# Feed-forward's first projection by seven block products in a float32 four-layer block

## The chip, the cores and the metric

One core of a Trainium2 chip runs one program. The time is device microseconds of that core for one execution, from a fixed set of inputs in device memory. An engine here is one of TensorE (PE, with its weight loads PEld), VectorE (DVE), ScalarE (ACT), GpSimd (POOL) and SyncE (SP), each with its own queue that is worked off in order; transfers are issued from such a queue too. TensorE's granted clock is 1.00 at 2.4 GHz and 0.50 at 1.2 GHz.

## The reference

The input is 512 tokens of 1024 channels. Four layers follow each other, each a mixer and a gated feed-forward with residuals and root-mean-square norms: a short convolution with forgetting attention, a conformer convolution, a gated recurrence in chunks, and windowed attention with sinks. The feed-forwards have the inner width 2816; layers 0 and 1 are plain, layers 2 and 3 put a causal convolution of three taps over the gate ahead of its silu.

```
def swiglu_ffn(h, w_ffn_in, w_ffn_out):
    g, u = jnp.split(h @ w_ffn_in, 2, axis=-1)
    return (jax.nn.silu(g) * u) @ w_ffn_out
```

All matrices are float32.

## The kernel before, in words

Every product of float32 matrices is made of three passes over float32r halves: each operand x is split into a high half (a ScalarE copy with rounding) and a low half (VectorE: x less the high half), and `mm3` (L539 to 541) adds high by high, high by low and low by high into one PSUM bank. The normed input lies transposed in `xh` and `xl` (8 blocks of 128 channels by 512 tokens).

Weights come as 379 units of 128 by 1024 numbers (512 KB) in the order of use: `w_dma` (issued at L484) loads a unit from SP's queue up to eight ahead, `w_hi` (L498, ScalarE) and `w_lo` (L507, VectorE) split it, and `get_w` hands the halves out. A unit of the up-projection holds all 1024 input channels of 128 output channels: `fm_unit` runs eight blocks of `mm3` with 512 token columns for it. Per feed-forward there are 22 pairs of such units (gate and value). The first two pairs go through `fm_quads(4)`: first the left 256 tokens of all four units, then the right 256, so that TensorE has work while the norm of the last token blocks is still under way. After each pair `epi` takes silu of the gate (L792, or L797 to L804 with the convolution), multiplies it with the value (L805) and splits the product (L530, L531) for the second projection, `out_proj`, which keeps TensorE busy for 22 more units.

At a stage's end `boundary` spawns for each of four token blocks the residual, the norm and `pre_norm`: ScalarE squares, VectorE scales, TensorE transposes (`xt`, L689), then the split into `xh` (L698) and `xl` (L699).

Nothing of the order is written by hand: each piece of work is a generator with a priority. A planner keeps a clock for each engine and takes at each step the operation that can start first, ties going to the smaller priority; its costs are in the code (`dve`, `act`, `pe`, `dma`, with `LAT` between engines). The order that it gives each engine is the order of that engine's queue on the chip. Buffers come from pools that the planner also counts: 34 slots of 4 KB a partition, 8 small tiles of 512 columns, 8 PSUM banks. Where the planner finds a hole of TensorE of over 0.6 us it puts in `warm` matmuls.

## Time and profile before

| | us |
|---|---|
| median of 3 runs (2326.45 to 2327.47) | 2326.93 |
| the profiled execution | 2326.68 |
| its span, first to last instruction | 2324.9 |
| TensorE busy | 2306.1 (99%) |
| VectorE busy | 1197.4 (52%) |
| ScalarE busy | 912.1 (39%) |
| POOL busy | 134.8 (6%) |

Stretches in the span: layer 0's feed-forward has its two plain pairs from 236 to 261 us, 20 pairs to 478.5, the second projection to 601; layers 1, 2 and 3 have the same stretches from 784, 1432 and 1955 us. Durations of single instructions overlap with their neighbours' on the same engine; the step from start to start is what one costs in a full queue. "[0.26 <-ACT wh L498]" behind a row says that the engine had been idle for 0.26 us and what released it.

### The profile page before, as it was taken

What the parts mean: (1) busy time and instruction counts of PE and PEld (TensorE: products, weight loads), DVE (VectorE), ACT (ScalarE), POOL (GpSimd) and SP (SyncE); (2) the same over time, 40 slices, a digit from 0 to 9 for tenths busy, and PEclk for the clock granted to TensorE, in tenths of its full rate; (3) what the DMA queues carried; (4) which work ended last, traced back from release to release, by engine and by line L of the source; (5) the groups of instructions that cost most, each with busy time, mean ns of one, the idle gap of its engine ahead of it and who ended that gap; (6) DMA issues with size and microseconds to landing.
All of it is one profiled execution on the core that took longest, in us unless ns stands there. A gap on an engine that the chain in (4) does not pass through costs nothing.

```text
span 2324.9 us, 29594 instructions
## 1 busy us (share of the span) xinstructions
PE 2306.1 (99%) x11888; PEld 1969.2 (85%) x11888; DVE 1197.4 (52%) x2038; ACT 912.1 (39%) x1614; POOL 134.8 (6%) x162
## 2 busy tenths in 40 slices
PE   9999999999999999999999999999999999999998
PEld 9888988888978988888888888888888998888887
DVE  5786433333687633333564875444434655444432
ACT  6454323222466322323443444333322664333321
POOL 0000000000284000000000000000000000000000
PEclk9999999999999999999999999999999999999999
DMA  4223322233333222234121214222243022222340
GB/s 179 101 82 118 119 73 91 81 128 107 120 138 126 91 91 76 90 106 154 73 73 64 73 47 135 91 73 77 96 163 109 19 90 93 91 73 76 105 137 36
DMA packets 62936, 224.68 MB, mean 97 GB/s; under 512 B 6984, under 2 KB 7240, under 8 KB 62800
## 3 DMA queue, kind: packets, MB, share of 16 engines
q1 hardware_dynamic: 62368, 222.41, 27.9%
q8 instruction: 93, 1.52, 0.3%
q10 hardware_dynamic: 432, 0.40, 0.1%
q14 instruction: 43, 0.35, 0.0%
HBM read 220.67 MB, written 2.11 MB: 96 GB/s over the span
## 4 chain that ended last, share of the span: by engine, by line
PE 95%; POOL 1%; DVE 1%; ACT 1%; issue 1%; DMA 0%; SPq 0%; POOLq 0%; ACTq 0%
PE fm L539 18%; PE fm L540 18%; PE fm L541 18%; PE op L539 9%; PE op L541 9%; PE op L540 9%; PE tm L539 2%; PE tm L541 2%; PE tm L540 2%; POOL cy L1190 1%; PE xt L689 1%; PE O L1745 1%; PE S L1508 1%; PE o L1571 1%; PE PT L1734 1%
## 5 line engine op out<-in xcount | busy, mean ns | idle before, releaser
L539 PE MATMUL fm<-xh,wh 128*128 128x512 f32 (+1 forms) x2160 | 794.8, 368 | 0.0
L540 PE MATMUL fm<-xl,wh 128*128 128x512 f32 (+1 forms) x2160 | 787.3, 364 | 0.2 <-DVE xl L699 0.2
L541 PE MATMUL fm<-xh,wl 128*128 128x512 f32 (+1 forms) x2160 | 787.3, 364 | 0.0
L507 DVE TENSOR_TENSOR wl<-wr,wh 128x1024 fp32r<-128x1024 f32 x379 | 457.4, 1232 | 287.2 <-ACT wh L498 182.3
L498 ACT ACTIVATE wh<-wr 128x1024 fp32r<-128x1024 f32 x379 | 387.6, 1052 | 264.0 <-DMA wr<-wall 138.5
L541 PEld LDWEIGHTS fm<-xh,wl 128*128 128x128 f32 x2160 | 407.9, 189 | 65.3
L539 PEld LDWEIGHTS fm<-xh,wh 128*128 128x128 f32 x2160 | 408.3, 189 | 61.7
L540 PEld LDWEIGHTS fm<-xl,wh 128*128 128x128 f32 x2160 | 408.3, 189 | 61.4 <-DVE xl L699 0.4
L539 PE MATMUL op<-wh,p 128*128 128x512 f32 x704 | 274.9, 390 | 0.4 <-DVE sg L805 0.4
L541 PE MATMUL op<-wh,p 128*128 128x512 f32 x704 | 274.0, 389 | 0.0
L540 PE MATMUL op<-wl,p 128*128 128x512 f32 x704 | 273.9, 389 | 0.0
L805 DVE TENSOR_TENSOR sg<-fm,sg 128x512 f32<-128x512 f32 x88 | 60.9, 692 | 383.2 <-PE fm L541 376.1
L530 ACT ACTIVATE p<-sg 128x512 fp32r<-128x512 f32 x88 | 55.6, 632 | 357.4 <-DVE sg L805 357.4
L539 PEld LDWEIGHTS op<-wh,p 128*128 128x128 f32 x704 | 132.1, 188 | 28.1 <-DVE sg L805 0.9
L541 PEld LDWEIGHTS op<-wh,p 128*128 128x128 f32 x704 | 132.1, 188 | 27.7
L540 PEld LDWEIGHTS op<-wl,p 128*128 128x128 f32 x704 | 132.2, 188 | 27.0
L660 POOL TENSOR_TENSOR ss<-ss,mhalf 128x1 f32<-128x1 f32 x48 | 26.0, 541 | 1417.1 <-DVE ss L655 1417.0
L539 PE MATMUL op<-wh,y 128*128 128x512 f32 x256 | 102.7, 401 | 0.2 <-DVE y L1004 0.2
L541 PE MATMUL op<-wh,y 128*128 128x512 f32 x256 | 100.0, 391 | 0.0
L540 PE MATMUL op<-wl,y 128*128 128x512 f32 x256 | 99.8, 390 | 0.0
L531 DVE TENSOR_TENSOR p<-sg,p 128x512 fp32r<-128x512 f32 x88 | 60.9, 692 | 61.4 <-ACT p L530 61.4
L1190 POOL TENSOR_TENSOR cy<-cp,cy 128x512 f32<-128x512 f32 x60 | 86.1, 1434 | 30.2 <-ACT cp L1189 26.3
(247 smaller groups left out, 2269.9 us busy)
## 6 DMA issues: line engine op xcount, KB each, us to landing
wr<-wall SPq DMA_DIRECT2D x379, 512.0 KB, 3.6
row<-rows SPq DMA_DIRECT2D x14, 512.0 KB, 3.9
cm<-cmat SPq DMA_DIRECT2D x14, 512.0 KB, 4.0
h<-x SPq DMA_DIRECT2D x8, 256.0 KB, 6.6
nck<-negc SPq DMA_DIRECT2D x4, 512.0 KB, 5.1
alibi<-alibi SPq DMA_DIRECT2D x4, 512.0 KB, 4.4
out<-out SPq DMA_DIRECT2D x8, 256.0 KB, 2.1
mk<-masks SPq DMA_DIRECT2D x2, 288.0 KB, 5.3
```

The lines of the kernel that those rows point to most:

```text
L498: yield act(1024, lambda: A.activation(out=b.t, in_=r.t, func=AF.Copy), (r,), (b,))
L507: yield dve(1024, lambda: V.tensor_tensor(out=b.t, in0=r.t, in1=hh.t.bitcast(F32), op=ALU.subtract), (r, hh), (b,))
L530: yield act(n, lambda: A.activation(out=y0, in_=raw, func=AF.Copy), (rb,), (yb,), psum=psum)
L531: yield dve(n, lambda: V.tensor_tensor(out=y1, in0=raw, in1=y0.bitcast(F32), op=ALU.subtract), (rb,), (yb,))
L539: T.matmul(out, lhsT=a[0], rhs=b[0], start=s, stop=False)
L540: T.matmul(out, lhsT=a[0], rhs=b[1], start=False, stop=False)
L541: T.matmul(out, lhsT=a[1], rhs=b[0], start=False, stop=e)
L660: yield Op("POOL", 0.29 + 0.167 * cols, lambda: G.tensor_tensor(out=ss[:, 8:8 + cols], in0=ss[:, 4:4 + cols], in1=mhalf[:, :cols], op=ALU. ...
L689: T.transpose(b[:, 128 * i:128 * i + 128], n[:, c:c + 128], ident)
L805: yield dve(512, lambda: V.tensor_tensor(out=c.t, in0=u.t, in1=c.t, op=ALU.mult), (u, c), (c,))
L1190: yield pool(512, lambda: G.tensor_tensor(out=y.t, in0=p.t, in1=y.t, op=ALU.add), (p,), (y,))
L1508: T.matmul(b[:, 128 * i:128 * i + 128].rearrange("p (j l) -> p j l", l=ln), lhsT=mix[:, 128 * i:128 * i + 128], rhs=dims(QP, 256 * i + ln, ...
```

## The change

In 20 of 22 pairs the product of a pair (gate and value, both 1024 channels by 128 outputs) with the input is treated as a product of two-by-two blocks: tokens in halves, channels in halves. Seven products of 512 channels by 256 tokens replace eight. Three of the seven need single weight blocks (11, 21, 22), four need sums of weight blocks (t1 to t4), and four need sums of input blocks, which `x_sums` makes at the start of each feed-forward from float32 copies that `keep` saves. `seven_sums` makes the weight sums in float32 and splits each of the seven: the first two sums come by one transfer from POOL's queue that adds 512 KB from DRAM (`wadd`) onto the unit in SBUF; the third sum is a VectorE addition, the fourth too in layers 0 and 1, and in layers 2 and 3 a second adding transfer of 256 KB. `pair` runs the products, `epi7` puts the outputs together from four PSUM banks, then comes `epi`. The product is now kept in float32 and split during the second projection (`halves`). Units of these pairs are loaded six ahead. The planner's price of `mm3` changes from 3 x 0.000422 a column to 3 x (0.0135 + columns / 2400) everywhere.

```diff
     def ffn(wi, wo):
         for m in range(NF):
-            us.append(_fm(wi, 128 * m))
-            us.append(_fm(wi, FF + 128 * m))
+            g, v = _fm(wi, 128 * m), _fm(wi, FF + 128 * m)
+            if m < N_PLAIN:
+                us.extend((g, v))
+            else:
+                us.append(np.concatenate([g[:, :512], v[:, :512]], 1))
+                us.append(np.concatenate([g[:, 512:], v[:, 512:]], 1))
...
+def weight_sums(a):
+    return np.stack([_fm(w, FF + 128 * m) for w in (a["w_ffn_in"][0], a["w_ffn_in"][1], a["ffn_w_up_2"][0], a["ffn_w_up_2"][1])
+                     for m in range(N_PLAIN, NF)])
...
+N_PLAIN = 2
+FFN_AT = (33, 33 + 3 * NF + 24, 33 + 6 * NF + 64, 33 + 9 * NF + 82)
+SEVEN = {u for f in FFN_AT for u in range(f + 2 * N_PLAIN, f + 2 * NF)}
+AHEAD_SEVEN = 6
...
     def w_dma():
         for u in range(N_UNITS):
             state["dma"] = u
-            yield Wait(lambda: u < W.cur + W.ahead_dma)
-            b = yield Alloc(spool, [128, 1024], F32, "wr", low=lambda: 4 if len(W.raw) > len(W.lo) + W.gone else 2)
-            yield dma(524288, lambda: nc.sync.dma_start(out=b.t, in_=ap["wall"][u]), (), (b,))
+            yield Wait(lambda: u < W.cur + (AHEAD_SEVEN if u in SEVEN else W.ahead_dma))
+            b = yield Alloc(spool, [128, 1024], F32, "wr", low=lambda: 1 if u in SEVEN else 4 if len(W.raw) > len(W.lo) + W.gone else 2)
+            yield dma(524288, lambda: nc.sync.dma_start(out=b.t, in_=ap["wall"][u]), (), (b,), lat=2.6 if u in SEVEN else 2.0)
             W.raw[u] = b
-
+            if u in SEVEN and u % 2 != SEVEN_ODD:
+                seven_sums(u - 1)
...
+    def seven_sums(u):
+        s1, s2 = W.raw[u], W.raw[u + 1]
+        f = max(i for i in range(4) if FFN_AT[i] <= u)
+        n = f * (NF - N_PLAIN) + (u - FFN_AT[f]) // 2 - N_PLAIN
+        subs = []
+        def part(s):
+            x = Buf(name="wsum", need=0)
+            x.w, x.weng = s.w, "DMA"
+            subs.append((s, x))
+            return x
+        l1, r1, l2, r2 = part(s1), part(s1), part(s2), part(s2)
+        left = [3]
+        lo_, hi_ = slice(0, 512), slice(512, 1024)
+        def piece(name, src, x):
+            b = yield Alloc(spool, [128, 2, 512], F32R, "w" + name, need=2, low=lambda: 0 if u < W.cur + 2 else 1)
+            yield act(512, lambda: A.activation(out=b[:, 0, :], in_=src, func=AF.Copy), (x,), (b,))
+            yield dve(512, lambda: V.tensor_tensor(out=b[:, 1, :], in0=src, in1=b[:, 0, :].bitcast(F32), op=ALU.subtract), (x,), (b,))
+            W.piece[u, name] = b
+        def end():
+            left[0] -= 1
+            if left[0] == 0:
+                for s, x in subs:
+                    s.r = max(s.r, x.r)
+                    s.w = max(s.w, x.w)
+                free(s1, s2)
+                W.gone += 2
+        def third():
+            yield from piece("t3", s1[:, hi_], r1)
+            end()
+        def first():
+            yield from piece("11", s1[:, lo_], l1)
+            yield Op("POOL", 1.0, lambda: G.dma_start(out=s1.t, in_=ap["wadd"][n], accum_op=ALU.add), (), (l1, r1), lat=6.5)
+            S.spawn(third(), prio, "sum3")
+            yield from piece("t1", s1[:, lo_], l1)
+            yield dve(512, lambda: V.tensor_tensor(out=s1[:, lo_], in0=s1[:, lo_], in1=s2[:, hi_], op=ALU.add), (r2,), (l1,))
+            yield from piece("t2", s1[:, lo_], l1)
+            if f > 1:
+                yield Op("POOL", 1.0, lambda: G.dma_start(out=s1[:, lo_], in_=ap["wall"][u + 1][:, lo_], accum_op=ALU.add), (), (l1,), lat=5.0)
+            else:
+                yield dve(512, lambda: V.tensor_tensor(out=s1[:, lo_], in0=s1[:, lo_], in1=s2[:, lo_], op=ALU.add), (l2,), (l1,))
+            yield from piece("t4", s1[:, lo_], l1)
+            end()
+        def second():
+            yield Wait(lambda: u < W.cur)
+            yield from piece("22", s2[:, hi_], r2)
+            yield from piece("21", s2[:, lo_], l2)
+            end()
+        def prio():
+            return -8 if u < W.cur + 2 else 1 + 0.001 * u
+        S.spawn(first(), prio, "sum1")
+        S.spawn(second(), prio, "sum2")
...
+    def pass3(n):
+        return 3 * (0.0135 + n / 2400.0)
...
+            if len(blocks) > 4:
+                S.spawn(keep(b, tb, kh, blocks[4]), -9.5 + tb, "keep")
+            else:
+                free(b)
...
+    def keep(b, tb, kh, raws):
+        if tb not in raws:
+            raws[tb] = yield slot((128, 2, 512), F32, "xr", need=2)
+        r = raws[tb]
+        yield act(512, lambda: A.activation(out=r[:, kh, :], in_=b.t, func=AF.Copy), (b,), (r,), psum=True)
+        free(b)
+    def x_sums(raws):
+        yield Wait(lambda: 2 in raws)
+        for i in range(4):
+            X.sums[i] = ((yield slot((128, 4, 256), F32R, "xs", need=2)), (yield slot((128, 4, 256), F32R, "xs", need=2)))
+        def one(t):
+            yield Wait(lambda: t in raws and t + 2 in raws)
+            a, b = raws[t], raws[t + 2]
+            x = yield t2("xd")
+            a11, a12, a21, a22 = a[:, 0, :], a[:, 1, :], b[:, 0, :], b[:, 1, :]
+            ba, bb, ts_ = Buf(name="xa", need=0), Buf(name="xb", need=0), slice(128 * t, 128 * t + 128)
+            def parts(i, src, rd):
+                h_, l_ = X.sums[i]
+                src = src.rearrange("p (k t) -> p k t", t=128)
+                oh, ol = h_[:, :, ts_], l_[:, :, ts_]
+                yield act(512, lambda: A.activation(out=oh, in_=src, func=AF.Copy), (rd,), (h_,))
+                yield dve(512, lambda: V.tensor_tensor(out=ol, in0=src, in1=oh.bitcast(F32), op=ALU.subtract), (rd, ), (l_,))
+            yield dve(512, lambda: V.tensor_tensor(out=x.t, in0=a11, in1=a21, op=ALU.subtract), (a, b), (x,))
+            yield dve(512, lambda: V.tensor_tensor(out=a21, in0=a21, in1=a22, op=ALU.subtract), (b,), (bb,))
+            yield dve(512, lambda: V.tensor_tensor(out=a22, in0=a21, in1=a11, op=ALU.subtract), (a, bb), (bb,))
+            yield dve(512, lambda: V.tensor_tensor(out=a12, in0=a12, in1=a22, op=ALU.add), (a, bb), (ba,))
+            yield from parts(0, a21, bb)
+            yield from parts(2, x.t, x)
+            free(x)
+            yield from parts(1, a22, bb)
+            yield from parts(3, a12, ba)
+            a.r = max(a.r, ba.r)
+            b.r = max(b.r, bb.r)
+            free(a, b)
+        for t in range(2):
+            S.spawn(one(t), -7, "xsum")
...
     def ffn(conv, R, chain_of):
-        ps = {}
-        spool.reserve += NF
+        at = W.cur
+        assert at in FFN_AT
+        pr, pp = {}, {}
+        left = [NF // 2]
+        spool.reserve += 1
+        def prod(b, cs, u, name, mov, rd):
+            yield Wait(lambda: (u, name) in W.piece)
+            w = W.piece.pop((u, name))
+            for k in range(4):
+                sl = slice(128 * k, 128 * k + 128)
+                yield pe(pass3(256), lambda: mm3(b[:, cs], (w[:, 0, sl], w[:, 1, sl]), mov(k), k == 0, k == 3), [w] + rd, [b])
+            free(w)
+        def block(half, kh):
+            ts_ = slice(256 * half, 256 * half + 256)
+            return (lambda k: (xh[:, 4 * kh + k, ts_], xl[:, 4 * kh + k, ts_])), [X.blocks[2 * half + i][kh] for i in range(2)]
+        def total(i):
+            a, b = X.sums[i]
+            return (lambda k: (a[:, k, :], b[:, k, :])), [a, b]
+        L_, R_ = slice(0, 256), slice(256, 512)
+        def pair(m):
+            u = at + 2 * m
+            yield Wait(lambda: (u, "11") in W.piece)
+            W.cur += 2
+            a = yield bank("fa", need=8)
+            yield from prod(a, L_, u, "11", *block(0, 0))
+            yield from prod(a, R_, u, "t1", *total(0))
+            b = yield bank("fb", need=8)
+            yield from prod(b, L_, u, "t3", *total(2))
+            yield from prod(b, R_, u, "22", *total(3))
+            d = yield bank("fd", need=4)
+            S.spawn(epi7(m, a, b, d, cs := []), -6, "epi7")
+            yield from prod(d, L_, u, "t2", *total(1))
+            c = yield bank("fc", need=8)
+            cs.append(c)
+            yield from prod(c, L_, u, "21", *block(0, 1))
+            yield from prod(c, R_, u, "t4", *block(1, 1))
+        def epi7(m, a, b, d, cs):
+            x = yield t2("x7", need=0)
+            v = yield t2("v7", need=0)
+            yield act(256, lambda: A.activation(out=x[:, L_], in_=a[:, L_], func=AF.Copy), (a,), (x,), psum=True)
+            yield dve(256, lambda: V.tensor_tensor(out=x[:, R_], in0=d[:, L_], in1=x[:, L_], op=ALU.add), (d, x), (x,))
+            free(d)
+            yield dve(256, lambda: V.tensor_tensor(out=v[:, L_], in0=a[:, R_], in1=x[:, R_], op=ALU.subtract), (a, x), (v,))
+            free(a)
+            yield dve(256, lambda: V.tensor_tensor(out=x[:, R_], in0=b[:, L_], in1=x[:, R_], op=ALU.add), (b, x), (x,))
+            yield dve(256, lambda: V.tensor_tensor(out=v[:, R_], in0=v[:, L_], in1=b[:, L_], op=ALU.subtract), (b, v), (v,))
+            yield dve(256, lambda: V.tensor_tensor(out=v[:, L_], in0=b[:, R_], in1=v[:, L_], op=ALU.add), (b, v), (v,))
+            free(b)
+            yield Wait(lambda: cs)
+            c = cs[0]
+            yield dve(512, lambda: V.tensor_tensor(out=x.t, in0=c.t, in1=x.t, op=ALU.add), (c, x), (x,))
+            free(c)
+            yield from epi(m, x, v)
...
-            yield dve(512, lambda: V.tensor_tensor(out=c.t, in0=u.t, in1=c.t, op=ALU.mult), (u, c), (c,))
-            free(u)
-            p = yield slot((128, 2, 512), F32R, "p", need=2)
-            spool.reserve -= 1
-            yield from split(c.t, c, (p[:, 0, :], p[:, 1, :]), p)
-            free(c)
-            ps[m] = p
-
-        bs = yield from fm_quads(4)
-        S.spawn(epi(0, bs[0], bs[1]), -5, "epi")
-        S.spawn(epi(1, bs[2], bs[3]), -5, "epi")
-        for m in range(2, NF):
-            g = yield from fm_unit()
-            u = yield from fm_unit()
-            S.spawn(epi(m, g, u), -5, "epi")
+            j = m // 2
+            if j not in pr:
+                pr[j] = None
+                pr[j] = yield slot((128, 2, 512), F32, "p", need=2)
+                left[0] -= 1
+                if left[0] < 1:
+                    spool.reserve -= 1
+            yield Wait(lambda: pr[j] is not None)
+            p = pr[j]
+            yield dve(512, lambda: V.tensor_tensor(out=p[:, m % 2, :], in0=u.t, in1=c.t, op=ALU.mult), (u, c), (p,))
+            free(u, c)
+        def halves():
+            for m in range(NF):
+                yield Wait(lambda: at + 2 * NF + m < W.cur + 3 and pr.get(m // 2) is not None)
+                p = pr[m // 2]
+                y = yield slot((128, 2, 512), F32R, "ph", need=2)
+                yield from split(p[:, m % 2, :], p, (y[:, 0, :], y[:, 1, :]), y)
+                pp[m] = y
+                if m % 2:
+                    free(p)
+        if len(X.blocks) > 4:
+            S.spawn(x_sums(X.blocks[4]), -7, "xsums")
+        bs = yield from fm_quads(2 * N_PLAIN)
+        for i in range(N_PLAIN):
+            S.spawn(epi(i, bs[2 * i], bs[2 * i + 1]), -5, "epi")
+        S.spawn(halves(), -5, "halves")
+        yield Wait(lambda: len(X.sums) == 4)
+        for m in range(N_PLAIN, NF):
+            yield from pair(m)
+        for i in range(4):
+            free(*X.sums[i])
+        X.sums.clear()
         chain, blocks = chain_of()
-        yield from out_proj([lambda m=m: ps.get(m) for m in range(NF)], chain, R)
+        yield from out_proj([lambda m=m: pp.get(m) for m in range(NF)], chain, R)
         X.blocks = blocks
```

## Rows read from the trace of the kernel before

**Rows 1.** The page, parts 1 and 4: busy time of TensorE, ending chain by engine.
```profile
PE 2306.1 (99%) x11888; PEld 1969.2 (85%) x11888; DVE 1197.4 (52%) x2038; ACT 912.1 (39%) x1614; POOL 134.8 (6%) x162
...
PE 95%; POOL 1%; DVE 1%; ACT 1%; issue 1%; DMA 0%; SPq 0%; POOLq 0%; ACTq 0%
```

**Rows 2.** Busy time by windows: us, each engine's us (instructions), granted clock, DMA share, GB/s.
```profile
236.00:261.00 25.00, 25.00 (x211) 24.96 (x210) 13.29 (x20) 10.60 (x19) 1.62 (x3) 1.00 0.44 148
261.00:478.50 217.50, 217.50 (x962) 180.09 (x961) 74.62 (x81) 62.71 (x80) 0.00 (x0) 1.00 0.26 87
478.50:601.00 122.50, 122.50 (x555) 101.65 (x554) 47.22 (x56) 36.69 (x56) 3.24 (x6) 1.00 0.33 110
...
1457.00:1674.50 217.50, 217.50 (x961) 180.10 (x961) 102.45 (x117) 79.04 (x100) 0.00 (x0) 1.00 0.24 83
...
1980.00:2197.50 217.50, 217.50 (x962) 180.09 (x962) 102.44 (x117) 77.46 (x98) 0.00 (x0) 1.00 0.25 84
```

**Rows 3.** Order of time, TensorE, 300.4 to 301.4 us: start, us; four more lie between.
```profile
300.21 0.39 PE L541 MATMUL fm<-xh,wl 128*128 128x512 f32 x1
...
301.35 0.39 PE L540 MATMUL fm<-xl,wh 128*128 128x512 f32 x1
```

**Rows 4.** Waits of 261 to 478.5 us: who, for whom, total us, times, longest.
```profile
DVE sg L805 <- PE fm L541: 119.4, 20, 6.2
...
DVE p L531 <- ACT p L530: 14.0, 20, 0.8
```

**Rows 5.** Order of time, TensorE: a half-width matmul, and the first full-width one after.
```profile
250.18 0.28 PE L539 MATMUL fm<-xh,wh 128*128 128x256 f32 x1
...
260.98 0.40 PE L539 MATMUL fm<-xh,wh 128*128 128x512 f32 x1
```

**Rows 6.** VectorE and ScalarE one by one: the input's split by tile, then order of time.
```profile
L699 DVE TENSOR_TENSOR xl<-xt,xh x64: 675/684/692, 11.4 to 1963.4; 128x512 fp32r<-128x512 f32 x64
...
225.53 1.28 DVE L699 TENSOR_TENSOR xl<-xt,xh 128x512 fp32r<-128x512 f32 x2
...
1190.05 0.41 DVE L1552 TENSOR_TENSOR QK<-QK,T 128x256 f32<-128x256 f32 x1
...
1191.05 0.76 DVE L1553 TENSOR_TENSOR QK<-QK,T 128x256 f32<-128x256 f32 x2
...
621.63 3.38 DVE L1164 SCALAR_TENSOR_TENSOR cy<-u,pf,cy 128x512 f32<-128x512 f32 x5
625.16 0.75 DVE L1134 SCALAR_TENSOR_TENSOR u<-fm,pf,sg 128x512 f32<-128x512 f32 x1
...
248.76 2.96 ACT L498 ACTIVATE wh<-wr 128x1024 fp32r<-128x1024 f32 x3
...
263.58 2.36 DVE L507 TENSOR_TENSOR wl<-wr,wh 128x1024 fp32r<-128x1024 f32 x2 [0.26 <-ACT wh L498]
```

**Rows 7.** Busy time by windows, columns as in rows 2: a stretch of the convolution module.
```profile
616.00:660.00 44.00, 44.00 (x233) 37.91 (x231) 39.96 (x56) 26.49 (x40) 31.04 (x23) 1.00 0.24 80
```

**Rows 8.** VectorE in order of time, and TensorE's waits over the span.
```profile
248.42 1.29 DVE L699 TENSOR_TENSOR xl<-xt,xh 128x512 fp32r<-128x512 f32 x2 [2.43 <-ACT xh L698]
...
PE fm L540 <- DVE xl L699: 0.2, 1, 0.2
```

**Rows 9.** The page, part 6: DMA issues, count, size, median us from issue to landing.
```profile
wr<-wall SPq DMA_DIRECT2D x379, 512.0 KB, 3.6
...
nck<-negc SPq DMA_DIRECT2D x4, 512.0 KB, 5.1
```

**Rows 10.** Windows around TensorE's longest wait, columns as in rows 2, and matmuls after it.
```profile
669.70:674.90 5.20, 0.02 (x1) 0.00 (x0) 2.70 (x4) 0.00 (x0) 4.96 (x5) 0.78 0.02 9
674.90:679.00 4.10, 4.08 (x12) 3.41 (x13) 2.50 (x7) 2.92 (x6) 0.90 (x2) 0.50 0.22 66
...
676.70 0.63 PE L541 MATMUL fm<-xh,wl 128*128 128x512 f32 x1
677.12 0.63 PE L539 MATMUL fm<-xh,wh 128*128 128x512 f32 x1
```

41 lines of the change are left out of this document (23 added, 18 removed).

## The prediction

> **What bounds the kernel now.** I read the page first: TensorE is busy for 99% of the span and the chain that ended last is 95% TensorE [rows 1]; VectorE has 52% and ScalarE 39%. Busy time of pipelined matmuls says little, so I looked at starts. In the first feed-forward's up-projection (261 to 478.5 us) the 512-column matmuls follow each other without a hole, 962 of them in the 217.50 us of that row [rows 2], 0.227 us from start to start [rows 3]. Nobody waits for VectorE there to the cost of TensorE: in the list of waits of this stretch VectorE and ScalarE wait for TensorE and for each other, and TensorE is on no line as a waiter [rows 4]. The third and fourth up-projections show the same row, 217.50 us filled, with VectorE busy 102.4 us there and 74.62 us in the first [rows 2]. So this stage is worth exactly its matmuls' spacing, and a change is worth what it takes off that spacing until another engine takes over. The profiled execution took 2326.68 us (span 2324.9 us), 0.25 below the median of the three runs; I sum against 2326.7.
>
> **TensorE's part.** The change leaves two of 22 channel pairs as they are and turns the other 20, in four layers, from 48 matmuls of 512 columns into 7 products x 4 blocks x 3 = 84 matmuls of 256 columns. The old pair costs 48 x 0.2266 = 10.88 us (217.5 us over 20 pairs [rows 2]). The price of a 256-column matmul stands in the trace, because the first two pairs already run in such halves: from 250.18 to 260.98 us there are 90 of them, 0.120 us each, with a weight load in front of every one [rows 5]. The new pair then costs 84 x 0.120 = 10.08 us. The gain is 0.80 us a pair, 7.3% instead of the 12.5% that seven for eight promises, since 84 matmuls pay the part that doesn't shrink with the columns (0.120 - 0.227/2 = 0.0065 us over half a long one) more often than 48. Over 80 pairs: 64 us. The bounds are narrow: 0.119 to 0.121 gives 57 to 71 us.
>
> The Trainium skill, VectorE: DVE Perf Modes, section "The TRN2 errata", prices a matmul at max(60, 6 + columns) cycles, which at the 2.4 GHz that the granted clock of 1.00 stands for is 0.216 and 0.109 us, and would make the gain 48 x 0.216 - 84 x 0.109 = 1.2 us a pair, an estimate of 97 us. The trace differs at both widths (0.227 and 0.120), and the measurement decides.
>
> **VectorE's part.** What a pair asks of it: seven differences of 512 columns (the low halves of the seven blocks), additions of weight blocks (two of 512 in layers 0 and 1, one in layers 2 and 3 where a second transfer replaces it), in the new epilogue five of 256 and one of 512, the product of 512, and in layers 2 and 3 the two convolution steps. It loses two differences of 1024 columns and the split of the product, which moves to the second projection (22 x 0.60 = 13 us a layer, under 122.5 us of matmuls in which VectorE is busy 47 us [rows 2]: nothing). Prices are steps between starts, not durations, since neighbours overlap: two of 512 columns from PSUM take 1.28 us with 0.684 for one, so 0.60 [rows 6]; 256 columns 0.34 (two in 0.76 with 0.41 for one [rows 6]); a step of the convolution's kind 0.66 (five in 3.38 with 0.75 for one [rows 6]). Layers 0 and 1: 7 x 0.60 + 2 x 0.60 + 5 x 0.34 + 0.60 + 0.60 = 8.3 us a pair, 82% of 10.08. Layers 2 and 3: 4.2 + 0.6 + 1.7 + 0.6 + 0.6 + 1.3 = 9.0 us, 89%. ScalarE has seven copies of 512 (about 0.5, half of a large one, three of which take 2.96 [rows 6]), a small one and one or two for the gate: 4.5 to 5.5 us, half the pair. So TensorE stays the bound, but by 1 to 2 us a pair instead of 5 to 7. Is 89% workable for an engine that takes its queue in order? One stretch shows it: from 616 to 660 us VectorE is busy 39.96 of 44 us and TensorE has no hole [rows 7]. There its work is long convolution sums from one buffer, here it is chains across ScalarE, so I don't take the waits as nothing. Bounds for layers 2 and 3: from 0 to 0.7 us a pair (below), I take 0.15, nearer the dense stretch: 40 x 0.15 = 6 us.
>
> The Trainium skill, VectorE: DVE Perf Modes, section "The TRN2 errata", also gives 120 + columns cycles at 0.96 GHz for a VectorE operation that reads PSUM, an estimate of 0.39 us for each of the five epilogue steps and 0.66 for the last, together 0.3 us a pair more, which would bring layers 2 and 3 to 9.3 us, 92%. The trace speaks for less: the pair of 512 columns from PSUM steps at 0.60, not 0.66.
>
> **The entry of each feed-forward.** New there, per layer: eight ScalarE copies that keep the transposed input in float32, four additions and four splits for each of two block rows, thus 16 x 0.60 = 9.6 us of VectorE and 16 x 0.5 = 8 us of ScalarE. They need the last block of the input, whose split ends at 249.7 us in layer 0, and the second product needs them 1.4 us after the plain pairs end at 260.98 [rows 5, 8]. In 236 to 261 us VectorE is busy 13.29 us and ScalarE 10.60 [rows 2]; with 9.6 for the sums and 5.4 for the first pair's blocks, less 4.9 us (three old weight differences and two splits) it comes to 23.4 of 25 us. It fits on paper, with nothing over. The copies and sums stand in the queues beside the norm of the last block; the second half of the plain pairs wants that block about when it is ready now (0.2 us of wait in the whole trace [rows 8]), so what delays it is paid at once. Behind a late sum on VectorE stand the epilogue of the plain pairs and the first pairs' blocks. Bounds per layer: 0 (all in the gaps) to 6 us (half of the sums, 4.8, and one copy pair, 1.0, in front of the norm). I take 2.5: 10 us.
>
> **The transfers.** Each pair adds a 512 KB accumulating transfer on POOL's queue (80 in all), and in layers 2 and 3 one of 256 KB (40). The trace has no accumulating transfer and none from POOL. Nearest rows: a plain 512 KB load lands after 3.6 us, the slowest kind of that size in the table after 5.1 [rows 9]; reading both operands doubles the shortest to 7.2. I take 5 to 7. A pair's blocks are loaded up to three pairs (30 us) ahead, and its chain (first block's split 1.2, transfer 7, split 1.2, addition 0.6, split 1.2, second transfer 6, split 1.2) is 18 us, so it hides; POOL is idle in the stage (0.00 us [rows 2]). Traffic goes from 1 MB in 10.9 us (83 to 87 GB/s, a quarter of the engines' time [rows 2]) to at most 1.75 MB in 10.1 us; layer 0's entry ran at 148 GB/s with 44%. Cover gone, one exposed landing costs 5 us at most. In order behind a block that waits for a landing on VectorE or ScalarE stand the epilogues, and TensorE needs their banks two pairs later. I put this at nothing beyond the 6 us above.
>
> **Sum.** 2326.7 - 64 + 10 + 6 = 2279 us. Its own range, from the ends above: 64 to 71 with nothing lost gives 2256 to 2263, and 57 with 24 for the entries gives 2294; I say 2260 to 2294.
>
> **Rivals.**
> - VectorE becomes the bound. In the old stage a low half waits 0.26 us for ScalarE's high half at the large blocks and 0.70 at the splits [rows 4, 6]. If each of the seven pays 0.26, 1.8 us, a pair takes 10.8 us in layers 2 and 3 (0.7 more than TensorE) and 10.1 in layers 0 and 1: 2326.7 - 64 + 10 + 40 x 0.7 = 2301 us. For: 89% load. Against: with some seven blocks ready to be made, another can be put into the gap, and the dense stretch. Range 2294 to 2322.
> - Slower: POOL's queue becomes a chain in layers 2 and 3. If it takes the two transfers of a pair in turn, the next pair's first one stands behind the second one, which waits for the first one's landing, two splits and an addition: landing + 1.2 + 0.7 + 1.2 + about 1 of issue. At a landing of 6 us that is 10.1 us, TensorE's own time; each further us costs 40 us. It decides at 7.2 us, where 40 x 1.2 = 48 us have eaten the 64 less 16; at 8 us it gives 2279 + 80 = 2359 us. For: nothing in the trace shows such a transfer's time. Against: the two belong to tasks of different pairs and the order is free to put the next pair's first one ahead. From 2331.
> - No gain seen: the sums at the entries and the waits together eat it to within 5 us, 2322 to 2331.
> - Seven for eight doesn't shorten TensorE at all: it would need 0.1295 us per short matmul, against 0.120 measured; under 1%.
>
> **How the numbers follow.** This kernel's runs agree to 0.04%, and a difference of about 0.2% (4.7 us) is what can be told from none. Forecast 62%, VectorE as bound 19%, slower 13%, no gain 6%. The range should hold 8 in 10: it takes in the forecast's own range and the VectorE case, 2256 to 2322. Faster 0.81, same 0.06, slower 0.13.
>
> **What would show it.** In the profile after: up-projections of about 203 to 208 us for the 20 pairs instead of 217.5, starts 0.120 us apart with the same granted clock; VectorE busy about 8 to 9 tenths there; holes of TensorE of a few us at the four entries, ended by the sums. Wrong would be: spacing above 0.125; TensorE waiting inside the stage for a block's low half (VectorE) or for the accumulating transfer; a lower granted clock after such waits, as after the 5.2 us hole at 669.7 us, behind which the clock row is 0.50 and matmuls start 0.43 us apart [rows 10].

## The result, and the profile after

The changed kernel takes 2294.6 us (median of 4 runs, 2291.39 to 2302.86) beside 2326.97 for the kernel before: a ratio of 0.9866, 95% interval 0.984 to 0.9892. That is faster, inside the predicted range, and 15.6 us above the predicted 2279. The profiled execution is the shortest of the four, 2291.39 us (span 2289.6), so the stages below are compared with that one: 35.3 us less span than before, where the sum had 48. One traced execution stands for each kernel below; times of whole kernels are medians.

From the page of the changed kernel (engine: busy us, share of the span, instructions; then the chain that ended last; and transfers with KB and median us to landing), to be held against [rows 1, 9]:

```profile
span 2289.6 us, 37731 instructions
PE 2256.5 (99%) x14816; PEld 2063.8 (90%) x14816; DVE 1654.2 (72%) x3102; ACT 1118.5 (49%) x2158; POOL 243.0 (11%) x282
PE 73%; DVE 10%; issue 6%; DMA 5%; POOL 3%; ACT 3%; POOLq 0%; SPq 0%; ACTq 0%; DVEq 0%
wr<-wall SPq DMA_DIRECT2D x379, 512.0 KB, 4.1
wr<-wadd POOLq DMA_DIRECT2D x80, 512.0 KB, 5.8
wr<-wall POOLq DMA_DIRECT2D x40, 256.0 KB, 4.7
```

TensorE is still busy for 99%, but of the chain it now holds 73% where it held 95%: VectorE, transfers and issue have come onto it.

Windows of the changed kernel, the same stretches as [rows 2] (columns: the stretch, its length, busy us and count of TensorE, its weight loads, VectorE, ScalarE and POOL, granted clock, share of the DMA engines, GB/s): the 20 pairs of layer 0, its second projection, the entry of layer 1, and the 20 pairs of layers 1, 2 and 3:

```profile
263.50:465.10 201.60, 201.60 (x1682) 201.60 (x1681) 172.54 (x313) 97.92 (x180) 14.66 (x17) 1.00 0.59 148
465.10:587.50 122.40, 122.40 (x554) 101.61 (x553) 59.51 (x77) 46.31 (x75) 3.26 (x6) 1.00 0.34 113
776.00:804.00 28.00, 27.45 (x228) 26.75 (x227) 25.71 (x43) 15.85 (x32) 3.58 (x5) 1.00 0.46 120
804.00:1005.50 201.50, 201.50 (x1681) 201.50 (x1681) 170.93 (x311) 96.46 (x178) 15.55 (x18) 1.00 0.59 145
1438.50:1649.40 210.90, 204.34 (x1682) 202.11 (x1681) 186.49 (x332) 112.93 (x201) 30.25 (x35) 1.00 0.69 160
1957.00:2163.00 206.00, 204.16 (x1683) 203.41 (x1682) 185.33 (x330) 109.38 (x196) 30.27 (x35) 0.99 0.71 165
```

Layers 0 and 1 are full: 1680 matmuls in 201.60 us, 0.120 us each at clock 1.00, with VectorE busy for 85%. Layers 2 and 3 issue as many matmuls, take 210.95 and 205.87 us from the first pair's first start to the second projection's first, and VectorE is busy 88 to 90% there. Added up from starts of matmuls:

| stretch | before | after | difference | in the sum |
|---|---|---|---|---|
| 20 pairs, layers 0 and 1 | 217.63 each | 201.60 each | -32.1 | -32 |
| 20 pairs, layers 2 and 3 | 217.63 each | 210.95, 205.87 | -18.4 | -26 |
| four entries (plain pairs) | 24.75, 24.75, 24.77, 24.75 | 25.73, 28.26, 23.89, 24.75 | +3.6 | +10 |
| mixers, from the projection before to the plain pairs | start to 236.22, 182.84, 283.55, 158.37 | to 237.81, 188.10, 286.65, 160.52 | +12.1 | 0 |
| second projections | 122.39 three times, 120.23 | 122.42 three times, 119.48 | -0.7 | 0 |

The differences add up to -35.5. The first line came as forecast. The rest of the text is mainly about the second and the fourth. "Holes" of a stretch of 20 pairs means below what it takes beyond 201.60 us: 9.4 us in layer 2 and 4.3 in layer 3.

What TensorE waits for, over the whole span (engine, tile and line that wait, what released them: us in total, times, longest):

```profile
PE cyT L1413 <- POOL u L1341: 4.9, 1, 4.9
PE fb L627 <- DVE w L528: 4.9, 6, 1.8
```

The first line is in the second mixer, and was there before. The second is inside the pairs and new: the second bank (`fb`) waits for the low half (`w`) of a block, which VectorE makes. The prediction had named this as a sign of being wrong. Waits for high or low halves at the bank `fc` come to another 3.3 us in all.

The entry of layer 1 shows no long wait, because the planner foresaw the hole and filled it with `warm` matmuls (VectorE and TensorE, from the timeline; rows between are left out):

```profile
787.12 1.41 DVE L767 SCALAR_TENSOR_TENSOR nx<-h,ss,row 128x512 f32<-128x512 f32 x2
789.44 2.39 PE L2094 MATMUL warm<-zeros 128*128 128x128 f32 x20
791.71 1.28 DVE L788 TENSOR_TENSOR xl<-xt,xh 128x512 fp32r<-128x512 f32 x2
792.45 0.39 PE L626 MATMUL fm<-xl,wh 128*128 128x256 f32 x1 [0.49 <-DVE xl L788]
```

The waits of the other engines in layer 2's pairs (1438.5 to 1649.4 us), which answer to [rows 4]:

```profile
POOL wr L552 <- DVE wt L528: 103.3, 16, 11.5
ACT wt L527 <- DMA wr<-wadd: 19.9, 11, 5.6
DVE wt L528 <- ACT wt L527: 13.1, 8, 3.8
ACT wt L527 <- DMA wr<-wall: 7.3, 6, 2.6
PE fb L627 <- DVE w L528: 4.6, 5, 1.8
```

Read from below: TensorE waits for VectorE, VectorE for ScalarE, ScalarE for the adding transfers. One hole in full, from the timeline of layer 2 (start us, duration, instruction, in brackets the idle time before it and its releaser; VectorE's rows between the second and the third are left out):

```profile
1570.10 0.63 ACT L527 ACTIVATE wt<-wr 128x512 fp32r<-128x512 f32 x1 [2.60 <-DMA wr<-wall]
1570.76 0.69 DVE L528 TENSOR_TENSOR wt<-wr,wt 128x512 fp32r<-128x512 f32 x1 [1.76 <-ACT wt L527]
...
1578.54 0.68 DVE L528 TENSOR_TENSOR w<-wr,w 128x512 fp32r<-128x512 f32 x1
1579.28 0.39 PE L627 MATMUL fb<-xs,w 128*128 128x256 f32 x1 [1.55 <-DVE w L528]
```

ScalarE stands 2.60 us for the second adding transfer, VectorE 1.76 us for ScalarE. Twelve VectorE instructions follow that one, with two gaps (0.94 and 0.16 us, both for ScalarE) in the 7.8 us up to 1578.54, and the last of them, the low half that TensorE needs, comes 1.55 us late. So a late landing passes through an engine that has no slack to catch up. This is a reading of one hole; the experiments take its two halves away one by one.

In layer 3 a second loss follows such a wait. TensorE stands 1.31 us for the high half of a block behind an adding transfer, then 0.23 us for its low half, and from 2130.6 to 2134.0 us its granted clock is 0.50, the lower level of 1.2 GHz (first the wait, then the window):

```profile
2129.26 0.39 PE L625 MATMUL fc<-xh,wt 128*128 128x256 f32 x1 [1.31 <-ACT wt L527]
2130.60:2134.00 3.40, 3.40 (x19) 3.40 (x18) 2.98 (x7) 0.26 (x1) 0.86 (x1) 0.50 0.24 23
```

Matmuls start 0.21 us apart there instead of 0.120; some 15 of them make about 1.4 of layer 3's 4.3 us. The prediction had named this too, a lower clock after a wait, and the sum has no term for it.

### The profile page after: what moved, and what is told of

Read it like the earlier page. It is cut to its first block, busy times and chain, and to the rows that moved or that the text cites. A ratio compares the mean times of both kernels' runs of the same rounds, so it can differ in the third digit from the quotient of the medians.

```text
span 2289.6 us, 37731 instructions
## 1 busy us (share of the span) xinstructions
PE 2256.5 (99%) x14816; PEld 2063.8 (90%) x14816; DVE 1654.2 (72%) x3102; ACT 1118.5 (49%) x2158; POOL 243.0 (11%) x282
## 4 chain that ended last, share of the span: by engine, by line
PE 73%; DVE 10%; issue 6%; DMA 5%; POOL 3%; ACT 3%; POOLq 0%; SPq 0%; ACTq 0%; DVEq 0%
PE op L626 8%; PE op L627 8%; PE op L625 8%; PE fm L625 5%; PE fm L626 5%; PE fm L627 5%; DMA wr<-wadd 3%; POOL cy L1402 2%; PE fc L627 2%; PE fa L625 2%; PE fa L627 2%; PE fa L626 2%; PE fb L627 2%; PE fb L626 2%; PE fb L625 2%
## 5 line engine op out<-in xcount | busy, mean ns | idle before, releaser
L625 PE MATMUL fm<-xh,wh 128*128 128x256 f32 (+1 forms) x880 | 298.1, 339 | 0.0
L626 PE MATMUL fm<-xl,wh 128*128 128x256 f32 (+1 forms) x880 | 289.7, 329 | 0.7 <-DVE xl L788 0.7
L627 PE MATMUL fm<-xh,wl 128*128 128x256 f32 (+1 forms) x880 | 289.6, 329 | 0.0
L625 PE MATMUL op<-wh,ph 128*128 128x512 f32 x704 | 274.7, 390 | 0.0
L627 PE MATMUL op<-wh,ph 128*128 128x512 f32 x704 | 274.0, 389 | 0.0
L626 PE MATMUL op<-wl,ph 128*128 128x512 f32 x704 | 273.9, 389 | 0.0
L528 DVE TENSOR_TENSOR wt<-wr,wt 128x512 fp32r<-128x512 f32 x320 | 217.2, 686 | 52.1 <-ACT wt L527 50.2
L627 PEld LDWEIGHTS fm<-xh,wl 128*128 128x128 f32 x880 | 167.8, 191 | 15.5
L626 PEld LDWEIGHTS fm<-xl,wh 128*128 128x128 f32 x880 | 168.2, 191 | 12.3 <-DVE xl L788 1.1
L625 PEld LDWEIGHTS fm<-xh,wh 128*128 128x128 f32 x880 | 168.1, 191 | 11.1
L627 PEld LDWEIGHTS op<-wh,ph 128*128 128x128 f32 x704 | 132.1, 188 | 27.7
L625 PEld LDWEIGHTS op<-wh,ph 128*128 128x128 f32 x704 | 132.2, 188 | 26.9
```

The lines of the kernel that those rows point to most:

```text
L528: yield dve(512, lambda: V.tensor_tensor(out=b[:, 1, :], in0=src, in1=b[:, 0, :].bitcast(F32), op=ALU.subtract), (x,), (b,))
L625: T.matmul(out, lhsT=a[0], rhs=b[0], start=s, stop=False)
L626: T.matmul(out, lhsT=a[0], rhs=b[1], start=False, stop=False)
L627: T.matmul(out, lhsT=a[1], rhs=b[0], start=False, stop=e)
```

## The experiments

Two questions: where the 12 us of the mixers come from, and whether the holes of layers 2 and 3 are made by VectorE's load alone, by the adding transfers alone (their traffic, POOL's queue, their late landing), or by both together. Lengths of 20 pairs are from start to start, as in the table. An experiment that leaves work out prices that work and is no kernel to use.

### The planner's price alone

The kernel before with nothing changed but the planner's price of three matmuls, `pass3` in the four places where the change puts it:

```diff
-        return pe(3 * 0.000422 * (hi - lo), lambda: mm3(...
+        return pe(pass3(hi - lo), lambda: mm3(...
...
-                    yield pe(0.648, lambda: mm3(...
+                    yield pe(pass3(512), lambda: mm3(...
```

> The kernel before with nothing changed but the planner's price of a three-pass product (3 x (0.0135 + columns / 2400) everywhere), so that only the order of the work changes. Of the changed kernel's 35 us gain, 50 stand in the four stretches of 20 pairs; about 11 us are given back outside the feed-forwards (conformer stretch 5, windowed attention 2, recurrence's end 3, first mixer 2). If the new price does that by re-ordering the other stages, this kernel is slower than before by about 10 us, 2337, with the loss in those stages. If the kept copies, sums and held buffers do it, this kernel is within 3 us of before.

Measured: 2335.85 us (2335.12 to 2337.12), ratio 1.0037 (1.0023 to 1.0052). The price alone costs some 8.5 us, and not in the pairs: 20 of them take 217.63 us as before. The second mixer, from the end of the second projection to the next plain pairs, in the kernel before, with the price alone, and in the changed kernel (windows):

```profile
601.00:783.84 182.84, 175.51 (x1028) 154.22 (x1027) 142.39 (x229) 103.78 (x173) 91.73 (x80) 0.98 0.36 123
```

```profile
603.17:788.69 185.52, 175.38 (x1028) 153.77 (x1026) 143.56 (x228) 104.01 (x173) 91.18 (x80) 0.99 0.36 121
```

```profile
587.56:775.66 188.10, 177.94 (x1027) 155.99 (x1026) 143.10 (x228) 105.79 (x177) 90.51 (x79) 0.97 0.35 117
```

The same counts of matmuls to within one, 2.7 us more by the price alone, and 2.6 more again in the changed kernel. The last 2.6 are not the change's: TensorE is busy 2.6 us longer for the same matmuls, at a mean clock of 0.97 instead of 0.99; a second stretch at the lower level lies at 710.6 to 714.1 us. Four executions below that keep the order of this stage (`drop_conv`, `drop_second`, `drop_first`, `plain_add`) have 0.99 and take 185.41 to 185.75 us, here with the plain copies:

```profile
587.45:772.86 185.41, 175.24 (x1027) 153.69 (x1026) 142.96 (x228) 105.82 (x177) 90.55 (x79) 0.99 0.36 119
```

TensorE's waits in this stretch, before and with the price alone:

```profile
PE cyT L1201 <- POOL u L1129: 5.2, 1, 5.2
PE cyT L1201 <- POOL cy L1190: 1.3, 1, 1.3
```

```profile
PE cyT L1204 <- POOL u L1132: 4.8, 1, 4.8
PE cyT L1204 <- POOL cy L1193: 2.9, 1, 2.9
PE cyT L1204 <- DVE cy L1175: 1.1, 1, 1.1
```

TensorE waits 8.8 us instead of 6.5 at the transposes of the convolution's output; the changed kernel has the same three waits, 4.9, 2.9 and 1.1. Over all four mixers the price costs 2.2 + 2.7 + 3.0 + 2.1 = 10.0 us, where the changed kernel has 12.1 (an entry that got 0.8 shorter makes the rest of the 9.2 of span).

### The change with the old price

The changed kernel, with the old prices for everything but the seven products:

```diff
-        return pe(pass3(hi - lo), lambda: mm3(...
+        return pe(3 * 0.000422 * (hi - lo), lambda: mm3(...
...
-                    yield pe(pass3(512), lambda: mm3(...
+                    yield pe(0.648, lambda: mm3(...
```

> The changed kernel with the old price of three-pass products for everything but the new 256-column products. If the new price costs the 11 us outside the feed-forwards, this runs at 2281 to 2285 us; if the kept copies and sums do, at about 2294 as the changed kernel, with the same stage lengths. The pair stretches should stay at 201.6, 201.6, 206 to 211, 206 to 211.

Measured: 2282.92 us (2277.79 to 2283.73), ratio 0.9805 (0.9791 to 0.982), 11.7 us under the changed kernel by the medians (7.6 by the traced executions) and the fastest of all that leave nothing out. The mixers take 4.4 us more than before instead of 12.1. The 20 pairs take 201.60, 201.60, 207.11 and 210.74 us. Windows of the last two:

```profile
1430.70:1637.80 207.10, 203.54 (x1682) 202.05 (x1681) 185.46 (x331) 109.17 (x196) 31.15 (x36) 1.00 0.72 164
1944.70:2155.40 210.70, 205.06 (x1682) 203.50 (x1681) 183.11 (x326) 108.72 (x195) 30.29 (x35) 0.99 0.70 161
```

So the holes stay: layer 3 now loses 9.1 us and layer 2 5.5, where it was 4.3 and 9.4 (layer 3 again with a stretch at the lower clock, from 2108.3 to 2111.7 us). Whether the order moved them isn't shown: it is one execution of each kernel, and four executions of the changed kernel lie up to 11.5 us apart.

### VectorE's load taken down

In layers 2 and 3 the two VectorE steps of the convolution are left out, the order stays:

```diff
-                yield dve(511, lambda: V.scalar_tensor_tensor(out=c[:, 1:], in0=g[:, :511], ...
-                yield dve(510, lambda: V.scalar_tensor_tensor(out=c[:, 2:], in0=g[:, :510], ...
+                yield dve(511, lambda: None, (g, bpf), (c,), aps=1)
+                yield dve(510, lambda: None, (g, bpf), (c,), aps=1)
```

> The changed kernel in the same order, without the two VectorE steps of the convolution in layers 2 and 3 (the gate is left unconvolved there): 1.3 us less VectorE work a pair. If the holes in those two stretches (9.4 and 4.3 us) come from VectorE's load, both stretches fall to 201.6 to 203 us and the kernel to about 2281. If they come from waiting for the second adding transfer's landing, holes of 4 us or more remain in each.

Measured: 2278.09 us (2275.53 to 2280.55), ratio 0.9789 (0.9774 to 0.9804). Layers 2 and 3 take 201.93 and 202.23 us. Window of layer 2:

```profile
1435.40:1637.30 201.90, 201.82 (x1682) 201.62 (x1681) 157.86 (x292) 112.62 (x201) 30.30 (x35) 1.00 0.72 168
```

With VectorE at 78% next to no hole is left (0.3 and 0.6 us), though all transfers run as before. The waits are even longer than in the changed kernel, where these two lines have 19.9 and 13.1 us, and yet they don't reach TensorE:

```profile
ACT wt L527 <- DMA wr<-wadd: 31.8, 14, 4.0
DVE wt L528 <- ACT wt L527: 31.2, 23, 3.9
```

The two steps are needed for the holes. They are also links of a chain (in the changed kernel ScalarE waits 25.6 us in layer 2 for the second one); this run takes load and chain away together.

### The second adding transfer left out

```diff
             if f > 1:
-                yield Op("POOL", 1.0, lambda: G.dma_start(out=s1[:, lo_], in_=ap["wall"][u + 1][:, lo_], accum_op=ALU.add), ...
+                yield Op("POOL", 1.0, lambda: None, (), (l1,), lat=5.0)
```

> The changed kernel in the same order, without the second adding transfer of layers 2 and 3 (the fourth weight sum lacks one term there); VectorE's work stays. If the holes come from waiting for that landing in ScalarE's and VectorE's queues, both stretches fall to 201.6 to 203 us and the kernel to about 2281. If VectorE's load alone makes them, they stay at 206 to 211 us and the kernel at 2290 to 2295.

Measured: 2289.51 us (2286.26 to 2292.27), ratio 0.9838 (0.9823 to 0.9852). Layers 2 and 3 take 207.57 and 207.67 us. That is 5.1 us under the changed kernel by the medians, but 6.0 and 6.1 us of holes stay, though POOL's queue holds one transfer a pair instead of two. Window of layer 2:

```profile
1436.30:1643.80 207.50, 203.58 (x1682) 201.96 (x1681) 186.07 (x332) 112.26 (x201) 14.68 (x17) 1.00 0.57 139
```

### The first adding transfer left out in layers 2 and 3

```diff
-            yield Op("POOL", 1.0, lambda: G.dma_start(out=s1.t, in_=ap["wadd"][n], accum_op=ALU.add), (), (l1, r1), lat=6.5)
+            yield Op("POOL", 1.0, (lambda: None) if f > 1 else (lambda: G.dma_start(...)), (), (l1, r1), lat=6.5)
```

> The changed kernel in the same order without the first adding transfer of layers 2 and 3 (the sums t1 and t3 lack a term there); the second one and all of VectorE's and ScalarE's work stay. Dropping the second alone left 6.0 and 6.1 us of holes. If the first transfer, on which three blocks of a pair hang, is what the full VectorE queue stands at, both stretches fall to 201.6 to 203 us. If either transfer is enough to make the holes, 204 to 208 stay.

Measured: 2280.72 us (2280.45 to 2284.82), ratio 0.9807 (0.9791 to 0.9824). Layers 2 and 3 take 203.68 and 202.53 us, with 2.1 and 0.9 us of holes. Windows:

```profile
1437.40:1641.10 203.70, 202.37 (x1683) 201.76 (x1682) 181.46 (x325) 107.36 (x194) 15.57 (x18) 1.00 0.47 121
1948.70:2151.30 202.60, 202.16 (x1683) 201.82 (x1682) 184.65 (x329) 108.77 (x197) 15.57 (x18) 1.00 0.46 122
```

VectorE is as full as in the changed kernel (184.65 of 202.6 us, 91%) and TensorE has few holes. Of the two it is the large transfer that matters more, 13.9 us by the medians for 5.1: the one that stands at the head of each pair's chain of sums.

### Both as plain copies

The same bytes from the same queue at the same places, copied over the buffer instead of added onto it:

```diff
-... G.dma_start(out=s1.t, in_=ap["wadd"][n], accum_op=ALU.add) ...
+... G.dma_start(out=s1.t, in_=ap["wadd"][n]) ...
-... G.dma_start(out=s1[:, lo_], in_=ap["wall"][u + 1][:, lo_], accum_op=ALU.add) ...
+... G.dma_start(out=s1[:, lo_], in_=ap["wall"][u + 1][:, lo_]) ...
```

> The changed kernel in the same order with both adding transfers as plain copies of the same bytes from the same queue (the weight sums then lack a term). It prices the adding itself: I expect the 512 KB transfer to land about 1.5 us earlier than the 5.6 to 6.6 us of the adding one, the 256 KB about 1 us earlier. If landings matter in layers 2 and 3, those stretches lose most of their 9.4 and 4.3 us of holes; if VectorE's load makes them, they stay within 3 us of drop_second's 207.6 each, kernel 2286 to 2292.

Measured: 2278.0 us (2275.73 to 2279.77), ratio 0.9788 (0.9774 to 0.9803). Layers 2 and 3 take 201.95 and 202.31 us. Window of layer 2, and behind it the two kinds from the page's table of transfers:

```profile
1435.40:1637.30 201.90, 201.80 (x1682) 201.60 (x1681) 184.64 (x330) 110.28 (x198) 18.81 (x35) 1.00 0.51 167
```

```profile
wr<-wadd POOLq DMA_DIRECT2D x80, 512.0 KB, 4.4
wr<-wall POOLq DMA_DIRECT2D x40, 256.0 KB, 3.0
```

VectorE is busy 184.64 of 201.9 us, 91%, and there is next to no hole (0.4 and 0.7 us). So at this load "the load alone" falls, as "the transfers alone" did with the convolution left out: both are needed. What the plain form changes is when the bytes are there: the 512 KB land after 4.4 us instead of 5.8 over the whole kernel, the 256 KB after 3.0 instead of 4.7. ScalarE's waits for them in layer 2 fall from 19.9 and 7.3 us to these:

```profile
ACT wt L527 <- DMA wr<-wadd: 2.5, 3, 1.6
ACT wt L527 <- DMA wr<-wall: 2.4, 2, 2.1
```

VectorE's idle time in front of the sums' low halves goes with them, as the groups by line say (first the changed kernel, then the plain copies):

```profile
L528 DVE TENSOR_TENSOR wt<-wr,wt 128x512 fp32r<-128x512 f32 x73 | 49.6, 686 | 13.7 <-ACT wt L527 13.1
```

```profile
L528 DVE TENSOR_TENSOR wt<-wr,wt 128x512 fp32r<-128x512 f32 x72 | 48.7, 683 | 0.8
```

The plain form also takes less of the DMA engines (0.51 for 0.69) and less of POOL (18.81 for 30.25 us). DMA share and lateness change together here. With the second transfer left out, though, the share fell to 0.57 and the holes stayed, and with the convolution left out it was 0.72 and there was next to none: the share alone doesn't make them. The waits for landings speak for the landing; no run changes it alone.

### The fourth sum by VectorE everywhere

```diff
-            if f > 1:
+            if f > 9:
                 yield Op("POOL", 1.0, lambda: G.dma_start(out=s1[:, lo_], ...
             else:
                 yield dve(512, lambda: V.tensor_tensor(out=s1[:, lo_], in0=s1[:, lo_], in1=s2[:, lo_], op=ALU.add), ...
```

> The changed kernel with the fourth weight sum by VectorE in all four layers: no second adding transfer, 0.6 us more VectorE work a pair in layers 2 and 3 (9.6 instead of 9.0 us by the prediction's sum, against 10.08 of TensorE). If VectorE's load makes the holes, the two stretches grow beyond 211 us, to 213 to 220, and the kernel to 2300 or more. If waiting for the second transfer had a large part, they stay at or below 206 to 211.

Measured: 2298.87 us (2295.88 to 2303.89), ratio 0.9881 (0.9866 to 0.9895). Layers 2 and 3 take 212.77 and 211.71 us, VectorE is busy for 93%:

```profile
1442.50:1655.20 212.70, 208.84 (x1714) 207.18 (x1713) 198.61 (x353) 115.50 (x202) 14.72 (x17) 0.99 0.54 139
```

Against the kernel without the second transfer, 2289.51, the fourth sum by VectorE costs 9.4 us, the second transfer 5.1. The change's choice, a second transfer in these two layers and VectorE in the others, looks the better one, but its 4.3 us of advantage aren't clear of noise: the runs of the two kernels overlap.

At 93% the load needs hardly any late landing. ScalarE waits only 3.7 us for transfers in the row, and the holes are 11.2 and 10.1 us. The planner foresaw part of them and filled it with 32 `warm` matmuls a layer, and in both layers a stretch of lower clock falls on them (0.68 in the mean from 1642.8 to 1648.2 us). So "both are needed" holds for the changed kernel's 88 to 91%, not beyond.

### Four attempts at a remedy

All four start from the change with the old price, 2282.92 us. The last step of the convolution as a ScalarE product and a POOL addition:

```diff
-                yield dve(510, lambda: V.scalar_tensor_tensor(out=c[:, 2:], ...
+                    yield act(510, lambda: A.activation(out=t[:, :510], in_=g[:, :510], func=AF.Copy, scale=pfc(cw, 3 * m)), ...
+                    yield pool(510, lambda: G.tensor_tensor(out=c[:, 2:], in0=t[:, :510], in1=c[:, 2:], op=ALU.add), (t,), (c,))
```

> The changed kernel with the old planner's price outside the new products, and in layers 2 and 3 the convolution's second step as a ScalarE product and a POOL addition in the 20 pairs: 0.66 us less VectorE work a pair, which brings it to the 8.3 us of layers 0 and 1, where no hole is seen. If load is the cause, both stretches fall to 201.6 to 203.5 us and the kernel to 2268 to 2272 (2282.9 less about 13). If something of these layers other than load is the cause (two transfers on POOL's queue, longer chains), holes of 4 us or more stay and the kernel at 2277 or more.

Measured: 2289.0 us (2286.81 to 2292.88), ratio 0.9838 (0.9822 to 0.9855). Layers 2 and 3 take 214.19 and 210.55 us: no better for 0.75 us less of VectorE a pair, which is busy for 84% of layer 2 now. By what was expected of it, the run speaks against the load as the whole cause. Groups by line in layer 2:

```profile
L528 DVE TENSOR_TENSOR wt<-wr,wt 128x512 fp32r<-128x512 f32 x73 | 57.5, 795 | 10.6 <-ACT wt L527 10.5
L999 POOL TENSOR_TENSOR sg<-cp,sg 128x510 f32<-128x510 f32 x19 | 22.5, 1186 | 58.0 <-ACT cp L998 46.1 <-DVE wt L528 5.4 <-DVE sg L991 4.5
```

The low halves of the sums take 795 ns instead of 686, 8 us in all, which eats more than half of the 14.2 us saved, and POOL's additions stand in the queue that issues the transfers. The Trainium skill, SBUF — State Buffer, section "Who interferes with whom", says that a VectorE instruction with two inputs in SBUF contends with a GpSimd instruction that reads SBUF. The rows fit that. These low halves have both inputs there; the 57 that no addition of POOL overlaps take 677 to 693 ns, and the 16 that one overlaps take 1195 in the mean, as here:

```profile
1506.82 1.08 POOL L999 TENSOR_TENSOR sg<-cp,sg 128x510 f32<-128x510 f32 x1 [2.60 <-DVE sg L991]
1507.03 1.43 DVE L528 TENSOR_TENSOR wt<-wr,wt 128x512 fp32r<-128x512 f32 x1 [0.38 <-ACT wt L527]
```

The chain got longer, too: ScalarE's silu now waits for POOL (9.9 us). What the slow halves, POOL's queue and the chain each cost isn't separated.

The transfers told to the planner as later than the change has them (7.0 and 6.5 for 6.5 and 5.0):

```diff
-... in_=ap["wadd"][n], accum_op=ALU.add), (), (l1, r1), lat=6.5)
+... in_=ap["wadd"][n], accum_op=ALU.add), (), (l1, r1), lat=7.0)
-... in_=ap["wall"][u + 1][:, lo_], accum_op=ALU.add), (), (l1,), lat=5.0)
+... in_=ap["wall"][u + 1][:, lo_], accum_op=ALU.add), (), (l1,), lat=6.5)
```

> old_price with the planner told that the adding transfers land later (7.0 us behind the issue instead of 6.5, the second one 6.5 instead of 5.0), so that VectorE and ScalarE take the blocks behind a transfer later in their queues. If the holes of layers 2 and 3 come from queues standing at a landing with VectorE too full to catch up, the stretches fall from 207.1 and 210.7 to 203 to 205 us each and the kernel from 2282.9 to 2272 to 2277. If the landings only show where the queue is late anyway, it stays within 3 us of 2283.

Measured: 2285.28 us (2283.1 to 2289.31), ratio 0.9825 (0.9811 to 0.984). Layers 2 and 3 take 209.67 and 210.75 us: an order made for a later landing has as many holes. Its runs overlap those of the old price.

VectorE's prices 2% up:

```diff
-        return Op("DVE", 0.069 + ...
+        return Op("DVE", 1.02*(0.069 + ...
```

> old_price with the planner's price of every VectorE operation 2% higher, landings as before: the order changes elsewhere too. If the holes come from a plan that fills VectorE tighter than the chip runs it, whatever the landings, the two stretches fall to 202 to 205 us; if the landings decide, at least one stays at 206 or more. Time of the kernel 2275 to 2290, since the other stages are re-ordered.

Measured: 2292.25 us (2289.72 to 2295.1), ratio 0.9855 (0.9838 to 0.9871). Layer 3 takes 203.55 us, layer 2 212.34, so an order that holds VectorE for slower doesn't do away with the holes. The mixers are re-ordered as well and take some 11 us more than before.

The blocks 22 and 21 a pair earlier in layers 2 and 3, the units loaded four ahead instead of six:

```diff
-AHEAD_SEVEN = 6
+AHEAD_SEVEN = 4
...
-            yield Wait(lambda: u < W.cur)
+            yield Wait(lambda: u < W.cur + (2 if f > 1 else 0))
```

> old_price, with the two single blocks of a pair's second unit (22 and 21) made one pair ahead in layers 2 and 3 instead of within their own pair, and units loaded four ahead instead of six to pay for the slots. In the changed kernel TensorE waits mostly for the low half of 22, which is queued on VectorE after its pair has begun. If that short lead is what turns VectorE's lateness into holes, the stretches of layers 2 and 3 fall to 202 to 205 us and the kernel from 2282.9 to 2272 to 2278. If VectorE's lateness reaches TensorE by whichever block is late, holes move to the other blocks and the time stays at 2280 to 2288.

Measured: 2292.3 us (2288.92 to 2295.75), ratio 0.9851 (0.9837 to 0.9866). The pairs take 202.47, 210.12, 211.29 and 209.67 us. Layer 1, which had no holes, has 8.5 us of them now with VectorE busy for 83%, and there only the shorter load distance is new. VectorE waits 27.7 us there for high halves of sums, where it was 11.3 with the old price: units loaded later leave the adding transfers less time, by this reading. So a load of 83% is no safety if the bytes come later still. The other half of the edit was not tried alone.

None of the four beats the old price. By the runs above a remedy would have to bring the first adding transfer's bytes earlier for the same VectorE work; that wasn't reached here.

## Why the prediction was right, and where 16 us went

The time lies in the stated range, but the sum was off by 15.6 us. The traced execution is 3.2 us shorter than the median, so 12.5 us can be placed by stage: 12.1 in the mixers and 7.6 in the pairs of layers 2 and 3, less 6.4 at the entries and 0.7 in the second projections. That the entries cost less than was taken is luck for the total.

**TensorE's part: right to the digit.** 84 matmuls at 0.120 us a pair, 16.03 us a layer, 64.1 us in all, seen bare in layers 0 and 1 and, with the transfers as plain copies, to 0.7 us in layers 2 and 3. The estimate of 97 us from the Trainium skill's price (VectorE: DVE Perf Modes, section "The TRN2 errata") does not hold for these matmuls: full stretches run at 0.120 us, not 0.109.

**VectorE's load: right; what it costs: too small.** Layers 0 and 1 at 85% lose nothing, layers 2 and 3 at 88 to 90% lose, as the step said. The term was mis-sized: 0.15 us a pair was taken, out of bounds of 0 to 0.7, and 9.4 + 4.3 = 13.7 us over 40 pairs makes 0.34 (some 1.4 of the 13.7 us is the lower clock in layer 3). It was taken near the dense stretch [rows 7], where VectorE works at 91% without a hole. With the plain copies the pairs do just that, so the load was only half of the question; in the dense stretch no engine's wait is ended by a transfer.

**The transfers: the step that failed inside the stage.** Their landing was bounded at 3.6 to 7.2 us and taken at 5 to 7; it is 5.8 and 4.7. What failed is "nothing beyond the 6 us above": the sum took the pairs' distance of 30 us as cover for a chain of 18 us. But it isn't TensorE that waits for a landing. ScalarE does, in order, 19.9 + 7.3 us in layer 2, and VectorE behind it 13.1. The prediction named the epilogues that stand behind such a wait; the price appeared at the blocks that stand there, mostly in VectorE's queue. Both signs of being wrong that the prediction named for this came: TensorE waits for low halves inside the stage, and once the clock falls behind such waits.

**Outside the feed-forwards: the step that was not there.** The diff says that the price of three matmuls changes everywhere, and the sum had no term for it. The order of the mixers changed. They take 12.1 us more. The price alone makes 10.0; of the 12.1, 2.6 are the second mixer's lower clock, which four executions of the same order don't have. The new price is nearer to the chip: it says 0.360 us for three matmuls of 256 columns and 0.680 for 512, as [rows 3, 5] have it; the old one 0.324 and 0.648. A truer number for one engine gave a worse order. Why, beyond where the waits moved, isn't settled; that it's the price is shown from both sides, by adding it alone (10.0 us of mixers) and by taking it out (7.7).

**The entries.** 10 us were taken, 0 to 6 each; +1.0, +3.5, -0.9 and 0.0 came, 3.6 in all. The mechanism of the step is seen in layer 1 alone, where VectorE is busy 25.71 of 28.00 us. There the last norm output (`nx`) and its low half (`xl`) stand on VectorE behind sums and first blocks, and TensorE pays with 2.2 us of `warm` matmuls and a wait of 0.49. The shorter entry of layer 2 comes with the price: it takes 23.98 us with the price alone.

**The second projection.** The splits moved there cost nothing: 122.42 us for 122.39, VectorE busy for 59.51.

**The rivals.** The median lies at the lower edge of the case "VectorE becomes the bound" (2294 to 2322) and just above the forecast's own range (to 2294), but not by that case's mechanism. It had every low half waiting 0.26 us for its high half; in layer 2 VectorE waits 13.7 us in front of 130 low halves, 0.1 each, and all of it at the sums, which stand behind a transfer. Without the mixers' 12 us the time would be well inside the forecast's own range, where the old price puts it (2282.9). POOL's queue as a chain did not happen: POOL waits for VectorE 103.3 us in layer 2, and with one transfer a pair instead of two holes of 6.0 and 6.1 us stay. "No gain" and "no shortening" fell with the 0.120 us.

## What to carry to other kernels

Where a planner orders the work, a changed price is an edit to every stage: give it a term of its own in the sum, and run it alone first. An in-order engine at 91% cost next to nothing here when what it works on was already there, at 93% it cost 10 to 11 us in each of two layers; ask for each input how late it can be, since without slack a late one is handed on to the bound engine. A stretch that shows a load to be workable is evidence only for inputs of the same kind.
